# The closing part of an MLP down projection: one row block finished ahead of the other, and a final RMSNorm whose square sums are added up ahead

## The chip, the cores and the metric

The kernel runs on one core of a Trainium2 chip. The metric is the device time of one execution in microseconds (us). The engines are named as in the profile: PE (TensorE), PEld (its weight loads), DVE (VectorE), ACT (ScalarE), POOL (GpSimd) and SP (SyncE, which only starts DMAs here); SPq, ACTq and POOLq are the queues on which these engines start DMAs.

## The reference, cut to what matters

A block of 256 tokens and 2048 channels passes a gated mixer (a linear recurrence beside a banded attention), then a squared-ReLU MLP of 8192 channels, then a last RMSNorm. All is float32. The change lies in the last two lines.

```python
h = h + mixer_block(rms_norm(h, norm_mix_w[l]), ...)
u = rms_norm(h, norm_mlp_w[l])
h = h + jnp.square(jax.nn.relu(u @ w_up[l])) @ w_down[l]
return rms_norm(h, norm_final_w)     # y * rsqrt(mean(y * y) + 1e-6) * w
```

## The kernel before

**Products.** Each float32 operand is split into a high and a low part (`wh`, `wl` for weights), and a product is three matmuls (L135, L136, L137 in `mm3`). The split of a piece of weights, 128x1024, is a cast on ACT (L91) and a subtraction on DVE (L92). The raw piece comes by a DMA on SP's queue (L688 in `piece`) into one of three kinds of buffers: `raw` (six of them), `rawd` (two), `rawp` (three). The split halves have five buffers each (`buf`). SP takes its DMAs in order, so one that waits for its buffer holds those behind it.

**Units.** The MLP is done as a row of `Unit`s. A unit computes two blocks of 512 output columns (n = 0, 1) for both blocks of 128 rows (m = 0, 1): four accumulators c11, c12, c21, c22 in PSUM. The first half of the contraction goes by a scheme with seven block products in place of eight (`product`; pieces A, B, C, D, with sums of raw pieces taken on DVE and by accumulating DMAs on POOL's queue), the second half by "plain" pieces of two contraction blocks each: `plain(n, ks)` for ks = (8,9), (10,11), (12,13), (14,15), each for both m. `LATE` are the last two of these. The order of a unit is written out in `run`; a scheduler places the instructions of every other engine around it.

**The last unit** is `dn32` (`tail=True`): output columns 1024 to 2047 of the down projection, the last quarter of its contraction. Its plain pieces of n = 0 go as in every unit: (12,13) for m = 0 and 1, then (14,15) for m = 0 and 1, then `u.end(0)` calls `done` for m = 0 and m = 1. The pieces of n = 1 then go in three steps: the first 256 columns of m = 1, all 512 of m = 0, the last 256 of m = 1, each step with both LATE pieces and followed by `done`.

**The last norm.** `done` is `out_of`. For the last quarter it adds the accumulator to the residual in `fin[m]` (`evict`, L717, DVE), squares it on ACT with the sum of squares into one column of `ssq3` (L1112, an ACTIVATE and a read of the accumulator), and for n below 3 multiplies by the norm's weights `wf` (L1114, DVE). Here n runs over four blocks of 512 columns; n = 0 and 1 come from unit `dn30`, n = 2 and 3 from `dn32`. When the last block of a row block m is there, DVE adds up the sums (L1118), turns them into a mean (L97), POOL raises it to the power -1/2 (L98), and four blocks are scaled: two on DVE (L1126, L1124, the latter with `wf`) and two on ACT (L1128). Each scaled block is written out by a DMA (L1129), two on SP's queue and two on ACT's.

`finals` (L1133, L1137) runs as a step of unit `dn30`. It loads `wf`, the norm's weights repeated over 128 partitions (1 MB), and the eight 256 KB blocks of the residual into `fin`, all on POOL's queue. In `dn30` ACT also copies the accumulator of product 21 twice (`u_dn`, L748), each time before PE adds to it again.

Of the kernel before, what the change touches and what calls it, by code (L numbers as in the profile page):

```python
# [8 lines left out]
F32 = mybir.dt.float32  # L9
# [3 lines left out]
ALU = mybir.AluOpType  # L13
# [3 lines left out]
P = 128  # L17
# [33 lines left out]
def tile_hybrid_block(  # L51
# [30 lines left out]

    mhalf = const.tile([P, 32], F32, name="mhalf")
    nc.gpsimd.memset(mhalf[:, 0:4], -0.5)
    room = small.tile([P, 56], F32, name="room", tag="room", bufs=1)
    nc.gpsimd.memset(room, 0.0)

    casts, marks = [], []
# [537 lines left out]
    def token(what, pool=None):  # L626
        if pool is not None:
            return pool.tile([P, NC], F32, name=what, tag="t2", bufs=8)
        return tk.tile([P, NC], F32, name=what, tag="t", bufs=TOK)
# [92 lines left out]
    class Unit:  # L722
# [13 lines left out]
        def load_item(self):  # L736

            n, ks = self.items.pop(0)
            self.raw[n, ks] = piece(self.w, f"{self.what}r{n}_{ks[0]}", self.n0 + n * NC, self.kt0 + ks[0], "rawp")

        def bank(self, i):

# [78 lines left out]
    def run(u, then=None):  # L821

        def q():
            if late:
                late.pop(0)()

        def item(x):
            if x and x.items:
                x.load_item()

        if not u.raw:
            u.load("A")
            u.load("B")
            u.load("C")
            u.load("D")
        for _ in range(3 - sum(type(k) is tuple for k in u.raw)):
            item(u)
        at = iter(range(99))
        u.bank("11")
        u.product("11", "A", u.block(0, 0), True)  # L840
        u.begun("21", "11")
        q()
        u.sums("A", "B")
        u.sent("B", "C")
        item(u)
        u.bank("22")
        u.product("22", "A", u.comb(5), True)
        u.begun("12", "22")
        q()
        item(u)  # L850
        u.steps = list(u.make_steps())
        u.step(next(at))
        u.product("12", "C", u.comb(4))
        u.step(next(at))
        u.product("11", "D", u.block(0, 1))
        with ExitStack() as es:
            if u.fresh:
                es.enter_context(tc.issue_after(lows[-1].ins))
            u.sums("A", "C")
        u.sent("D", "A")  # L860
        u.step(next(at))
        u.plain(1, (8, 9))
        item(u)
        u.step(next(at))
        u.product("21", "A", u.comb(2))
        u1 = u.copy(token(f"u1_{u.what}"), "21")
        if then:
            then.load("A")
        u.step(next(at))
        u.plain(1, (10, 11))  # L870
        u.less("12", u1)
        item(u)
        u.step(next(at))
        u.product("21", "B", u.comb(7))
        u2 = u.copy(token(f"u2_{u.what}"), "21")
        if then:
            then.load("B")
            then.load("C")
        u.step(next(at))
        u.plain(0, (8, 9))  # L880
        u.less("22", u2)
        item(u)
        u.step(next(at))
        u.plain(0, (10, 11))
        item(u)
        u.step(next(at))
        u.product("21", "D", u.block(1, 1))
        if then:
            then.load("D")
        u.step(next(at))  # L890
        u.plain(0, (12, 13))
        item(u)
        u.step(next(at))
        u.plain(0, (14, 15))
        marks.clear()
        item(then)
        u.end(0)
        while u.steps:
            u.step(99)

        if u.tail:
            halves = [u.plain(1, ks, ()) for ks in LATE]
            for m, c in ((1, slice(0, T)), (0, slice(0, NC)), (1, slice(T, NC))):
                for h in halves:
                    h(m, c)
                u.done(m, 1, u.c["12"[m] + "2"], c)
            return

        def rest():
            u.plain(1, LATE[1])  # L910
            u.end(1)

        late.append(lambda: u.plain(1, LATE[0]))
        late.append(rest)
# [146 lines left out]
        nc.gpsimd.dma_start(hd[n][m], t)  # L1061
        h1[n][m] = t

    ssq3 = small.tile([P, NM, 5], F32, name="ssq3", tag="ssq3", bufs=1)
    ssum3 = small.tile([P, NM], F32, name="ssum3", tag="ssum")
    rstd3 = const.tile([P, NM], F32, name="rstd3")
    NQ = 4
# [3 lines left out]
    for qd in range(NQ):  # L1071
        last = qd == NQ - 1
        uT, rs, Su, blocks = [], {}, {}, {}

        def turns(c0, uT=uT, rs=rs, Su=Su, blocks=blocks, qd=qd):

            def one(c, m):
                if not m:
                    uT.append(new_act(f"u{qd}{c}"))
                hi, lo = uT[c][:, :, 0, :], uT[c][:, :, 1, :]  # L1080
                tp = transpose4(rs[c, m], f"u{qd}{c}{m}")
                if c < 2:
                    blocks[m, c] = fours(token(f"a{m}{c}_u{qd}"))
                    nc.scalar.copy(blocks[m, c], tp)
                split(hi[:, :, m * P:(m + 1) * P], lo[:, :, m * P:(m + 1) * P], tp)

            return [(c, lambda c=c, m=m: one(c, m)) for c in (c0, c0 + 1) for m in range(NM)] + [
                (c0 + 1, f, 7) for f in ([] if c0 else combos(uT, f"u{qd}", tk, Su, blocks))]

        for c in range(0, 4, 2):  # L1090
            def done(m, n, acc, c=c, rs=rs, qd=qd):
                t = token(f"r{qd}{c}{n}{m}")
                with tc.high_priority(offset=2000):
                    nc.scalar.activation(t, acc, AF.Relu, scale=rstd2[:, m:m + 1])
                nc.scalar.activation(t, t, AF.Square)
                rs[c + n, m] = t

            units.append(Unit(lambda: hT, lambda: Sh, w_up, qd * (FF // NQ) + c * NC, f"up{qd}{c}", done,
                              steps=(lambda turns=turns: turns(0)) if c else (lambda: ()) if qd else (lambda: h_blocks(2)), start=3 if c else 0))

        def out_of(m, n, acc, c=slice(0, NC), last=last, qd=qd):
            if not last:
                t = token(f"y{qd}{n}{m}")
                with tc.high_priority(offset=2000):
                    nc.scalar.copy(t, acc)  # L1105
                nc.gpsimd.dma_start(hd[n][m], t, accum_op=ALU.add)  # L1106
                return
            wf = fin["w"]
            r = fin[m][:, n * NC:(n + 1) * NC]
            evict(r[:, c], acc[:, c])  # L1110
            j = n + (c.start > 0)
            nc.scalar.activation(token(f"ysq_{j}_{m}")[:, c], r[:, c], AF.Square, accum_out=ssq3[:, m, j:j + 1])  # L1112
            if n < 3:
                nc.vector.tensor_tensor(r, r, wf[:, n * NC:(n + 1) * NC], op=ALU.mult)  # L1114
                return
            if c.stop < NC:
                return
            nc.vector.tensor_reduce(ssum3[:, m:m + 1], ssq3[:, m, 0:j + 1], axis=AX.X, op=ALU.add)  # L1118
            rsqrt(rstd3[:, m:m + 1], ssum3[:, m:m + 1], D, 1)
            f = rstd3[:, m:m + 1]  # L1120
            for i in (2, 0, 3, 1):
                t = fin[m][:, i * NC:(i + 1) * NC]
                if i == 3:
                    nc.vector.scalar_tensor_tensor(t, t, f, wf[:, i * NC:(i + 1) * NC], op0=ALU.mult, op1=ALU.mult)  # L1124
                elif i == 2:
                    nc.vector.tensor_scalar(t, t, f, None, op0=ALU.mult)  # L1126
                else:
                    nc.scalar.activation(t, t, AF.Copy, scale=f)  # L1128
                (nc.sync if i > 1 else nc.scalar).dma_start(out[m * P:(m + 1) * P, i * NC:(i + 1) * NC], t)  # L1129

        def finals():
            fin["w"] = apool.tile([P, D], F32, name="wf", tag="act")
            nc.gpsimd.dma_start(fin["w"], bass.AP(tensor=norm_final_w.tensor, offset=norm_final_w.offset, ap=[[0, P], [1, D]]))  # L1133
            for m in range(NM):
                fin[m] = apool.tile([P, D], F32, name=f"fin{m}", tag="act")
                for n in range(4):
                    nc.gpsimd.dma_start(fin[m][:, n * NC:(n + 1) * NC], hd[n][m])  # L1137

        for n0 in (0, 2):
            units.append(Unit(lambda uT=uT: uT, lambda Su=Su: Su, w_down, n0 * NC, f"dn{qd}{n0}",  # L1140
                              lambda m, n, acc, *c, n0=n0, out_of=out_of: out_of(m, n0 + n, acc, *c), kt0=qd * KD,
                              steps=(lambda: ()) if n0 else (lambda turns=turns, last=last: turns(2) + [(3, finals)] * last),
                              start=0, tail=last and n0 == 2))
# [47 lines left out]
```

## Time and profile before

| | us |
|---|---|
| time, median of 3 runs (lowest to highest) | 1399.73 (1399.07 to 1400.38) |
| time of the profiled execution | 1399.67 |
| its span, first to last instruction | 1398.0 |
| PE busy in the span | 1381.4 (99%) |
| DVE, ACT, POOL busy | 1138.2, 922.3, 143.8 |
| first matmul of `dn32`'s plain pieces (12,13) of n = 0 | at 1376.28 |
| last matmul begins | at 1387.21 |

The profiled execution's time stands 1.67 us above its span. Times of single instructions are counted from the span's start. A row of the timeline gives start, duration, engine, line, operation and tiles, how many were merged, and in brackets how long the engine had been idle and what released it. Matmuls overlap: one of 512 columns is shown with 0.39 us, but the next begins 0.23 us after it.

### The profile page before, as it was taken

To read this page: it belongs to the slowest core of one execution; us is meant where nothing else is said; L and a number is where in the kernel's file an instruction comes from. 1 tells how busy PE (TensorE), PEld (TensorE's weight loads), DVE (VectorE), ACT (ScalarE), POOL (GpSimd) and SP (SyncE) were. 2 spreads that over 40 slices of the span, in tenths; PEclk is the share of its full clock that TensorE was granted. 3 is DMA by queue.
4 is the path that set the end of the run, shared out by engine and by line. 5 is a ranking of instruction groups with operands and counts; after the bars stand their busy time and mean duration, and the time that the engine had idled before them with its cause. 6 is when DMAs were issued, how large, how long until landed. Compare 5 with 4: busy or idle time off the path is not lost.

```text
span 1398.0 us, 18644 instructions
## 1 busy us (share of the span) xinstructions
PE 1381.4 (99%) x6550; PEld 1144.4 (82%) x6550; DVE 1138.2 (81%) x1431; ACT 922.3 (66%) x1192; POOL 143.8 (10%) x228
## 2 busy tenths in 40 slices
PE   9999999999999999999999999999999999999997
PEld 7889888878777888888888888888888888888885
DVE  7897997976978785687998987889877888879885
ACT  6774764665676674346777776778666876668764
POOL 2000001010100000001211001100011001010200
PEclk9999999999999999999999999999999999999999
DMA  9755455775769897658988889998899888999883
GB/s 318 242 168 161 154 166 181 225 269 162 183 187 271 251 278 225 193 169 268 283 244 275 252 268 267 274 280 240 249 295 299 248 230 254 281 279 275 267 245 114
DMA packets 124078, 331.62 MB, mean 237 GB/s; under 512 B 11072, under 2 KB 11840, under 8 KB 123600
## 3 DMA queue, kind: packets, MB, share of 16 engines
q1 hardware_dynamic: 103264, 264.80, 55.1%
q0 software_dynamic: 19568, 64.04, 23.3%
q10 hardware_dynamic: 1152, 1.60, 0.4%
q8 instruction: 51, 0.84, 0.2%
q14 instruction: 43, 0.35, 0.1%
HBM read 271.67 MB, written 10.49 MB: 202 GB/s over the span
## 4 chain that ended last, share of the span: by engine, by line
PE 90%; DVE 4%; DMA 3%; issue 1%; ACT 1%; POOL 0%; SPq 0%; POOLq 0%; ACTq 0%; DVEq 0%
PE acc_ak L177 2%; PE acc_aq L177 2%; PE acc_hf L177 2%; PE ps L414 1%; PE acc_ak L182 1%; PE acc_hq L177 1%; PE tp_u L108 1%; PE acc_ga0c L135 1%; PE acc_hg L136 1%; PE acc_bb L136 1%; PE acc_hg L135 1%; PE acc_ba L136 1%; PE acc_bb L137 1%; PE acc_ba L137 1%; PE acc_hg L137 1%
## 5 line engine op out<-in xcount | busy, mean ns | idle before, releaser
L177 PE MATMUL acc_hf<-act_x,wh_hf 128*128 128x512 f32 x128 | 41.0, 402 | 1.0 <-DVE f L190 1.0
L177 PE MATMUL acc_aq<-act_x,wh_aq 128*128 128x512 f32 x128 | 41.6, 406 | 0.0
L177 PE MATMUL acc_hq<-act_x,wh_hq 128*128 128x512 f32 x128 | 40.7, 399 | 0.0
L177 PE MATMUL acc_ak<-act_x,wh_ak 128*128 128x512 f32 x128 | 40.0, 396 | 0.1
L91 ACT CAST wh_bb<-raw_bb 128x1024 fp32r<-128x1024 f32 x16 | 16.9, 1054 | 23.3 <-PE acc_ba L137 17.7
L92 DVE TENSOR_TENSOR wl_bb<-raw_bb,wh_bb 128x1024 fp32r<-128x1024 f32 x16 | 19.6, 1223 | 14.8 <-ACT wh_bb L91 14.8
L91 ACT CAST wh_ba<-raw_ba 128x1024 fp32r<-128x1024 f32 x16 | 16.8, 1052 | 20.9 <-PE acc_bb L137 13.8
L92 DVE TENSOR_TENSOR wl_ba<-raw_ba,wh_ba 128x1024 fp32r<-128x1024 f32 x16 | 19.6, 1223 | 12.6 <-ACT wh_ba L91 12.6
L91 ACT CAST wh_aq<-raw_aq 128x1024 fp32r<-128x1024 f32 x16 | 16.8, 1050 | 19.0 <-PE acc_hg L137 8.8
L92 DVE TENSOR_TENSOR wl_aq<-raw_aq,wh_aq 128x1024 fp32r<-128x1024 f32 x16 | 19.6, 1223 | 11.4 <-ACT wh_aq L91 9.4
L182 PEld LDWEIGHTS acc_hq<-act_x,wl_hq 128*128 128x128 f32 x128 | 23.4, 188 | 6.1 <-DVE wl_hq L92 0.9
L182 PEld LDWEIGHTS acc_hf<-act_x,wl_hf 128*128 128x128 f32 x128 | 23.4, 188 | 6.1 <-DVE wl_hf L92 0.9
L182 PEld LDWEIGHTS acc_aq<-act_x,wl_aq 128*128 128x128 f32 x128 | 23.5, 188 | 5.4 <-issue 0.5
L182 PEld LDWEIGHTS acc_ak<-act_x,wl_ak 128*128 128x128 f32 x128 | 23.5, 188 | 5.3
L92 DVE TENSOR_TENSOR wl_hf<-raw_hf,wh_hf 128x1024 fp32r<-128x1024 f32 (+2 forms) x21 | 20.3, 967 | 7.8 <-ACT wh_hf L91 7.7
L91 ACT CAST wh_hf<-raw_hf 128x1024 fp32r<-128x1024 f32 (+1 forms) x19 | 16.9, 890 | 14.3 <-PE acc_hg L137 6.0
L182 PE MATMUL acc_aq<-act_x,wl_aq 128*128 128x256 f32 x128 | 25.9, 284 | 0.0
L92 DVE TENSOR_TENSOR wl_ak<-raw_ak,wh_ak 128x1024 fp32r<-128x1024 f32 x16 | 19.5, 1221 | 7.7 <-ACT wh_ak L91 7.7
L135 PE MATMUL acc_hi<-wh_hi,act_x 128*128 128x512 f32 x64 | 25.8, 403 | 0.0
L92 DVE TENSOR_TENSOR act_u<-tp_u,act_u 128x512 fp32r<-128x512 f32 x32 | 21.9, 685 | 4.7 <-ACT act_u L91 4.2
L135 PE MATMUL acc_hg<-wh_hg,act_x 128*128 128x512 f32 x64 | 25.7, 401 | 0.0
L1106 POOL DMA_DIRECT2D hd<-y x24 | 25.4, 1137 | 1.9 <-ACT y L1105 1.8
(1922 smaller groups left out, 5248.0 us busy)
## 6 DMA issues: line engine op xcount, KB each, us to landing
raw_hi<-in_w_in_n_dram SPq DMA_DIRECT2D x16, 512.0 KB, 4.4
raw_hg<-in_w_in_n_dram SPq DMA_DIRECT2D x16, 512.0 KB, 3.9
raw_aq<-in_w_in_t_dram SPq DMA_DIRECT2D x16, 512.0 KB, 4.3
raw_ak<-in_w_in_t_dram SPq DMA_DIRECT2D x16, 512.0 KB, 3.8
raw_ba<-in_w_branch_a_dram SPq DMA_DIRECT2D x16, 512.0 KB, 4.5
raw_bb<-in_w_branch_b_dram SPq DMA_DIRECT2D x16, 512.0 KB, 4.6
raw_hf<-in_w_in_t_dram SPq DMA_DIRECT2D x12, 512.0 KB, 3.9
raw_hq<-in_w_in_t_dram SPq DMA_DIRECT2D x12, 512.0 KB, 4.4
```

The lines of the kernel that those rows point to most:

```text
L91: casts[:] = [(copy or nc.scalar.copy)(hi, src)]
L92: return nc.vector.tensor_tensor(lo, src, hi.bitcast(F32), op=ALU.subtract)
L108: nc.tensor.transpose(tp[:, j, :], src[:, j * P:(j + 1) * P], ident)
L135: nc.tensor.matmul(acc, hi, wh, start=first, stop=False, skip_group_check=True)
L136: nc.tensor.matmul(acc, hi, wl, start=False, stop=False, skip_group_check=True)
L137: nc.tensor.matmul(acc, lo, wh, start=False, stop=last, skip_group_check=True)
L177: nc.tensor.matmul(acc[:, cb, :], wh[:, cb * P:(cb + 1) * P], r.rearrange("p u t -> p (u t)"), start=kt == 0, stop=last)
L182: nc.tensor.matmul(acc[:, cb, 0:T], wl[:, cb * P:(cb + 1) * P], r[:, 0, :], start=False, stop=False)
L414: nc.tensor.matmul(ps[:, m, :], klf[:, a * P:(a + 1) * P], qrf[:, a * 192:(a + 1) * 192], start=True, stop=True)
L1106: nc.gpsimd.dma_start(hd[n][m], t, accum_op=ALU.add)
```

## The change

In the last unit the four LATE pieces, two of n = 0 and two of n = 1, are all split ahead, and then PE goes in five steps: n = 0 for m = 0, n = 1 for m = 0, the first 256 columns of n = 1 for m = 1, n = 0 for m = 1, the last 256 columns of n = 1 for m = 1. Each step takes its two LATE pieces and ends in `done`. So m = 0 is complete after the second step; its scaling and its writes stand between the work of m = 1 on ACT's, DVE's and SP's queues.

The two LATE raw pieces of n = 1 go into `raw` buffers, and their loads stand ahead of the last three `rawp` loads on SP's queue.

`ssq3` has one more column, set to 2048 * 1e-6 by POOL near the start of the kernel. The sums of squares that are there when block n = 2 is done are added up then (DVE), and POOL adds the last one and takes the power itself. The mean step on DVE goes. Since the factor is now (sum + 2048 eps)^(-1/2), the weights `wf` are multiplied once by the square root of 2048, on ACT, in unit `dn30`: ACT's order has it (128x2048) right in front of the first `u_dn` copy.

Seven of the eight output writes go on SP's queue; the last one, block 1 of m = 1, on ACT's. `room` is a filler that keeps the addresses of the small tiles. PE has the same matmuls as before.

```diff
         def load_item(self):
             n, ks = self.items.pop(0)
-            self.raw[n, ks] = piece(..., "rawp")
+            self.raw[n, ks] = piece(..., "raw" if self.tail and n and ks in LATE else "rawp")
...
         u.product("21", "D", u.block(1, 1))
         if then:
             then.load("D")
+        if u.tail:
+            ends = [[u.plain(n, ks, ()) for ks in LATE] for n in range(2)]
+            for m, n, c in ((0, 0, slice(0, NC)), (0, 1, slice(0, NC)), (1, 1, slice(0, T)), (1, 0, slice(0, NC)), (1, 1, slice(T, NC))):
+                for h in ends[n]:
+                    h(m, c)
+                u.done(m, n, u.c["12"[m] + "12"[n]], c)
+            return
+
...
-        if u.tail:
-            halves = [u.plain(1, ks, ()) for ks in LATE]
-            for m, c in ((1, slice(0, T)), (0, slice(0, NC)), (1, slice(T, NC))):
-                for h in halves:
-                    h(m, c)
-                u.done(m, 1, u.c["12"[m] + "2"], c)
-            return
...
             evict(r[:, c], acc[:, c])
-            j = n + (c.start > 0)
+            j = n + 1 + (c.start > 0)
             nc.scalar.activation(token(f"ysq_{j}_{m}")[:, c], r[:, c], AF.Square, accum_out=ssq3[:, m, j:j + 1])
+            if n == 2:
+                with tc.high_priority(offset=3000):
+                    nc.vector.tensor_reduce(ssum3[:, m:m + 1], ssq3[:, m, 0:4 + m], axis=AX.X, op=ALU.add)
             if n < 3:
                 nc.vector.tensor_tensor(r, r, wf[:, n * NC:(n + 1) * NC], op=ALU.mult)
-                return
-            if c.stop < NC:
-                return
-            nc.vector.tensor_reduce(ssum3[:, m:m + 1], ssq3[:, m, 0:j + 1], axis=AX.X, op=ALU.add)
-            rsqrt(rstd3[:, m:m + 1], ssum3[:, m:m + 1], D, 1)
-            f = rstd3[:, m:m + 1]
+            elif c.stop == NC:
+                f = rstd3[:, m:m + 1]
+                nc.gpsimd.tensor_tensor(f, ssq3[:, m, j:j + 1], ssum3[:, m:m + 1], op=ALU.add)
+                nc.gpsimd.tensor_tensor(f, f, mhalf[:, 0:1], op=ALU.pow)
...
-                (nc.sync if i > 1 else nc.scalar).dma_start(out[m * P:(m + 1) * P, i * NC:(i + 1) * NC], t)
+                    (nc.scalar if m and i == 1 else nc.sync).dma_start(out[m * P:(m + 1) * P, i * NC:(i + 1) * NC], t)
 
         def finals():
+            nc.gpsimd.memset(ssq3[:, :, 0:1], D * EPS)
             fin["w"] = apool.tile([P, D], F32, name="wf", tag="act")
             nc.gpsimd.dma_start(fin["w"], ...)
+            nc.scalar.activation(fin["w"], fin["w"], AF.Copy, scale=D ** 0.5)
```

More of the change, by code (lines that the diff above doesn't have):

```diff
@@ L84, in tile_hybrid_block @@
     nc.gpsimd.memset(mhalf[:, 0:4], -0.5)
-    room = small.tile([P, 56], F32, name="room", tag="room", bufs=1)
+    room = small.tile([P, 88], F32, name="room", tag="room", bufs=1)
     nc.gpsimd.memset(room, 0.0)
@@ L738, in load_item @@
             n, ks = self.items.pop(0)
-            self.raw[n, ks] = piece(self.w, f"{self.what}r{n}_{ks[0]}", self.n0 + n * NC, self.kt0 + ks[0], "rawp")
+            self.raw[n, ks] = piece(self.w, f"{self.what}r{n}_{ks[0]}", self.n0 + n * NC, self.kt0 + ks[0],
+                                    "raw" if self.tail and n and ks in LATE else "rawp")
         def bank(self, i):
@@ L1062, in h_out @@
         h1[n][m] = t
-    ssq3 = small.tile([P, NM, 5], F32, name="ssq3", tag="ssq3", bufs=1)
+    ssq3 = small.tile([P, NM, 6], F32, name="ssq3", tag="ssq3", bufs=1)
     ssum3 = small.tile([P, NM], F32, name="ssum3", tag="ssum")
@@ L1116, in out_of @@
-            if c.stop < NC:
-                return
-            nc.vector.tensor_reduce(ssum3[:, m:m + 1], ssq3[:, m, 0:j + 1], axis=AX.X, op=ALU.add)
-            rsqrt(rstd3[:, m:m + 1], ssum3[:, m:m + 1], D, 1)
-            f = rstd3[:, m:m + 1]
[L1121 to L1129, printed above, removed]
+            elif c.stop == NC:
+                f = rstd3[:, m:m + 1]
+                nc.gpsimd.tensor_tensor(f, ssq3[:, m, j:j + 1], ssum3[:, m:m + 1], op=ALU.add)
+                nc.gpsimd.tensor_tensor(f, f, mhalf[:, 0:1], op=ALU.pow)
+                for i in (2, 0, 3, 1):
+                    t = fin[m][:, i * NC:(i + 1) * NC]
+                    if i == 3:
+                        nc.vector.scalar_tensor_tensor(t, t, f, wf[:, i * NC:(i + 1) * NC], op0=ALU.mult, op1=ALU.mult)
+                    elif i == 2:
+                        nc.vector.tensor_scalar(t, t, f, None, op0=ALU.mult)
+                    else:
+                        nc.scalar.activation(t, t, AF.Copy, scale=f)
+                    (nc.scalar if m and i == 1 else nc.sync).dma_start(out[m * P:(m + 1) * P, i * NC:(i + 1) * NC], t)
```

## The prediction

> **What bounds the kernel now.** I read the page first: how long the span is, who is busy, and the chain that ended last.
>
> ```profile
> span 1398.0 us, 18644 instructions
> PE 1381.4 (99%) x6550; PEld 1144.4 (82%) x6550; DVE 1138.2 (81%) x1431; ACT 922.3 (66%) x1192; POOL 143.8 (10%) x228
> PE 90%; DVE 4%; DMA 3%; issue 1%; ACT 1%; POOL 0%; SPq 0%; POOLq 0%; ACTq 0%; DVEq 0%
> ```
>
> PE sets the time nearly everywhere, and the change gives it the same matmuls. So there are two questions: does PE still run without a gap up to its last matmul, and how long is what follows it? That end I read in the timeline, from the last two evictions on.
>
> ```profile
> 1381.92 0.69 DVE L717 TENSOR_TENSOR fin<-acc_dn32c,fin 128x512 f32<-128x512 f32 x1 [0.67 <-PE acc_dn32c L137]
> 1386.10 0.69 DVE L717 TENSOR_TENSOR fin<-acc_dn32c,fin 128x512 f32<-128x512 f32 x1 [1.72 <-PE acc_dn32c L137]
> 1387.21 0.28 PE L137 MATMUL acc_dn32c<-wh_dn32r,act_u 128*128 128x256 f32 x1
> 1387.53 0.42 DVE L717 TENSOR_TENSOR fin<-acc_dn32c,fin 128x256 f32<-128x256 f32 x1 [0.74 <-PE acc_dn32c L137]
> 1387.87 0.14 DVE L1118 TENSOR_REDUCE ssum<-ssq 128x1 f32<-128x4 f32 x1
> 1388.29 0.58 POOL L98 TENSOR_TENSOR rstd<-ms,mhalf 128x1 f32<-128x1 f32 x1 [31.86 <-DVE ms L97]
> 1388.31 0.19 ACT L1112 ACTIVATION_READ_ACCUMULATOR ysq<-fin 128x1 f32 x1
> 1388.90 1.33 ACT L1128 ACTIVATE fin<-fin,rstd 128x512 f32<-128x512 f32 x2 [0.41 <-POOL rstd L98]
> 1389.30 0.75 DVE L1124 SCALAR_TENSOR_TENSOR fin<-fin,rstd,wf 128x512 f32<-128x512 f32 x1
> 1389.41 3.06 SPq L1129 DMA_DIRECT2D out_dram<-fin  x4
> 1389.96 0.15 DVE L1118 TENSOR_REDUCE ssum<-ssq 128x1 f32<-128x5 f32 x1
> 1390.15 0.15 DVE L97 TENSOR_SCALAR ms<-ssum 128x1 f32<-128x1 f32 x1
> 1390.38 0.55 POOL L98 TENSOR_TENSOR rstd<-ms,mhalf 128x1 f32<-128x1 f32 x1 [1.52 <-DVE ms L97]
> 1390.97 1.33 ACT L1128 ACTIVATE fin<-fin,rstd 128x512 f32<-128x512 f32 x2 [0.74 <-POOL rstd L98]
> 1390.97 0.49 DVE L1126 TENSOR_SCALAR fin<-fin,rstd 128x512 f32<-128x512 f32 x1 [0.67 <-POOL rstd L98]
> 1391.72 0.99 ACTq L1129 DMA_DIRECT2D out_dram<-fin  x2
> ```
>
> The two row blocks end together. The last eviction of m = 0 is at 1386.10, that of m = 1 at 1387.53. The reduction of m = 0 stands behind that eviction on DVE (1387.87), so its factor is used only from 1388.90. The last sum of squares of m = 1 is read at 1388.31 + 0.19 = 1388.50, but DVE is busy scaling m = 0 until its reduction can go at 1389.96; mean and power follow, and m = 1 is scaled from 1390.97. I call the time from which a row block is scaled U: U was 1388.90 for m = 0, 1390.97 for m = 1. All eight writes start after 1389.4. The next view is their landing, for the first one and for the last two, and the DMA busy share and rate from 1388 to 1399 in 40 slices of 0.275 us.
>
> ```profile
> L1129 SPq DMA_DIRECT2D out_dram<-fin x1: 344/344/344, 1389.4 to 1389.4; - x1
> DMA to landing us min/median/max: 2.3/2.3/2.3
> L1129 SPq DMA_DIRECT2D out_dram<-fin x1: 332/332/332, 1392.1 to 1392.1; - x1
> L1129 ACTq DMA_DIRECT2D out_dram<-fin x1: 373/373/373, 1392.3 to 1392.3; - x1
> DMA to landing us min/median/max: 4.6/4.6/4.6
> DMA  0000000079999999999999999998540000000000
> GB/s 0 0 0 0 0 0 0 0 276 402 410 410 402 387 320 425 387 395 395 343 320 231 350 395 365 328 395 313 216 156 8 0 0 0 0 0 0 0 0 0
> DMA packets 1152, 2.10 MB, mean 191 GB/s; under 512 B 128, under 2 KB 128, under 8 KB 1152
> ```
>
> The first write needed 2.3 us, the last 4.6 us: the DMA engines are full from slice 8 (1390.2) to slice 28 and empty at 1396.3. So the writes of m = 1 queue behind those of m = 0. The last lands at 1392.3 + 4.6 = 1396.9, 0.6 us after the last packet, and the span ends 1.1 us after that, at 1398.0, which is U + 7.03 for m = 1.
>
> **The change part by part.** *PE's order.* PE does the same matmuls. Before it finished n = 0 for both m (24 matmuls of 512 columns, 0.23 us apart, as the 5.6 us from 1376.28 to the eviction at 1381.92 show) before it needed the LATE pieces of n = 1; now it needs them after 12, at 1376.28 + 2.7 = 1379.0. The last subtractions of those pieces:
>
> ```profile
> 1374.84 2.60 DVE L92 TENSOR_TENSOR wl_dn32r<-rawp_dn32r,wh_dn32r 128x1024 fp32r<-128x1024 f32 x2 [1.49 <-ACT wh_dn32r L91]
> 1350.60 1.22 DVE L92 TENSOR_TENSOR wl_dn32p12C<-raw_dn32C,wh_dn32p12C 128x1024 fp32r<-128x1024 f32 x1
> 1357.15 14.68 SPq L688 DMA_DIRECT2D rawp_dn32r<-in_w_down_dram  x5
> ```
>
> They end at 1377.44, 1.6 us early: cost nothing, and should the cover go, PE slips by what exceeds 1.6. That also holds for the raw loads, which now go into `raw` buffers ahead of three `rawp` loads in SP's order. The `raw` buffers that they take are those of piece C, last read by the subtraction at 1350.60 to 1351.82; the `rawp` load behind them started at 1357.15. So SP is through 5 us early and holds nothing back. PE's end stays: 1387.5.
>
> *The end of m = 0.* Its last eviction comes 24 matmuls after 1376.28, where m = 1's n = 0 was evicted before: 1381.92, not 1386.10. From the start of an eviction to the read sum took 1387.53 to 1388.50 for 256 columns, about 1.4 for 512; with add and power on POOL U is near 1384.3. ACT's two scalings (1.33) end near 1385.7 and stand ahead of m = 1's squares in ACT's queue, DVE's two (0.49 and 0.75) near 1385.5 ahead of its evictions: the next to be late would be the eviction at 1386.10, so both fit. Four writes of m = 0 are done by about 1389.5, before m = 1 begins to write.
>
> *The end of m = 1.* The reduction moves to 1387.87, beside the square; the mean (0.15) goes; the wait for DVE behind m = 0 goes. POOL gets an add. No row shows an add on POOL; the nearest are these.
>
> ```profile
> L84 POOL MEMSET mhalf<- 128x4 f32 x1 | 0.1, 101 | 0.0
> 141.53 0.69 POOL L98 TENSOR_TENSOR ro<-ms,mhalf 128x2 f32<-128x2 f32 x1 [2.98 <-DVE ms L97]
> 740.45 1.22 DVE L92 TENSOR_TENSOR wl_up00r<-rawp_up00r,wh_up00r 128x1024 fp32r<-128x1024 f32 x1
> 740.62 1.61 POOL L98 TENSOR_TENSOR rstd<-ms,mhalf 128x2 f32<-128x2 f32 x1 [13.18 <-DVE ms L97]
> ```
>
> Its bounds are 0.10 (a memset) and 0.58 (the power); I take 0.20, nearer to the memset, since the power's extra work is what an add lacks. Chain: read at 1388.50, 0.09 to POOL (as from the mean's end, 1388.20, to 1388.29), add 0.20, 0.05 between them, power 0.55, 0.03 to ACT: U = 1389.42, against 1390.97, 1.55 earlier.
>
> Beside it DVE multiplies m = 1's block 2 by `wf`, about 1387.95 to 1388.65. The power took 0.69 with DVE idle and 1.61 beside a DVE subtraction of two SBUF operands; here only the first 0.07 us of the add lies beside one, so I price that at 0.05, inside the bounds. The Trainium skill says as much against this change: in its GPSIMD Engine Reference, Specifications, GpSimd's SBUF interfaces are shared with VectorE and contend with VectorE instructions that have two SBUF inputs. The 1.61 agrees; by that rule U would be later by what the multiplication overlaps.
>
> *The writes.* The first transfer of m = 0 began 1.3 after its U (1390.2). For m = 1 the issue order gives the same start, then 1.05 MB, half the 2.10, at the 395 GB/s of slices 9 to 18 takes 2.65, landing 0.6, end 1.1: U + 5.65 in place of U + 7.03, 1.4 less. That three of its writes share SP's queue costs nothing, since an issue takes 0.34 and its transfer 0.66.
>
> *`wf` on ACT.* One activation of 128x2048, ahead of the copy that PE's product 21 B waits for.
>
> ```profile
> L1133 POOL DMA_DIRECT2D wf<-in_norm_final_w_dram x1: 588/588/588, 1310.5 to 1310.5; - x1
> DMA to landing us min/median/max: 11.4/11.4/11.4
> L212 ACT ACTIVATE xr<-xr 128x2048 f32<-128x2048 f32 x2 | 3.8, 1920 | 1.6 <-DMA xr<-in_x_dram 1.6
> 1322.08 0.59 ACT L748 COPY u_dn<-acc_dn30c 128x512 f32<-128x512 f32 x1 [0.30 <-PE acc_dn30c L137]
> 1324.60 0.39 PE L135 MATMUL acc_dn30c<-wh_dn30p21B,S_u 128*128 128x512 f32 x1
> DMA to landing us min/median/max: 10.9/13.9/15.9
> ```
>
> `wf` lands at 1321.9. ACT then scales for 1.92, to 1323.9, and copies for 0.59, to 1324.5; PE needs the copy at 1324.60. It just fits: I charge 0.1, between 0 and 0.4. What is queued behind on ACT are casts for matmuls that PE comes to only after 21 B. POOL's memset of the new column, 0.1, comes near the start and delays nobody.
>
> Sum: -1.55 - 1.4 + 0.05 + 0.1 = -2.8. Span 1395.2, with the 1.67 outside it 1396.9; the profiled execution stands 0.06 under the median of 1399.73, which I let go. A measurement of this kernel can tell about 0.2%, 2.8 us, from no change: the line lies at 1396.93, on the forecast itself.
>
> **The rivals.** *Quicker writes.* If m = 1's last write, issued at U + 1.37, lands like the first one of before, in 2.3 to 3.0, the end is U + 4.8 to 5.5: 1394.2 to 1394.9, time 1395.9 to 1396.6. For it: the queues are empty then. Against it: 1.05 MB needs 2.65 anyhow.
>
> *POOL's pair is slow, or m = 1's writes gain nothing from an empty queue.* An add of 0.58 and a power stretched to 1.0 beside DVE put U at 1390.2; or the writes need as long as m = 0's did (its last landing 5.3 after U, at 1394.2). Either gives back 0.7 to 0.8: 1397.7. For it: the 1.61. Against it: DVE is idle during the power.
>
> *The change trades the end for a stall in `dn30`, slower than before.* The mechanism is `wf`'s landing: ACT waits for it in order, with the copy and all casts behind. PE slips one for one beyond 0.15 us of slack. The eight loads queued right behind `wf` took 10.9 to 15.9 us. If `wf` takes 15.9 in place of 11.4, PE loses 4.35 and the time is 1396.9 + 4.3 = 1401.2. It decides from a landing of 14.4 us on. Against it: nothing ahead of `wf` changes.
>
> *The change does not do what it says*: the last pieces of n = 1 are late at 1379.0, PE waits, and m = 0 ends no earlier. It needs the 1.6 us of cover to go; 1397.5 at one us beyond. I leave it in the second rival.
>
> **How the numbers follow.** Forecast 0.46, its own range 1396.2 to 1397.6 from the add's bounds (-0.1, +0.4) and the stall's (0 to 0.4), half on each side of the line; quicker writes 0.29, all faster; slow POOL or slow writes 0.16, all within; late `wf` 0.09, of which 0.05 past 1402.5 (a landing of over 17 us, beyond the rows) and 0.04 within. Faster 0.23 + 0.29 = 0.52, same 0.23 + 0.16 + 0.04 = 0.43, slower 0.05. The range leaves out the late `wf` and the outermost of the quick writes: 1395.6 to 1398.6.
>
> **What would show it.** Right: PE's last matmul still near 1387.2; m = 0's last eviction near 1381.9, its writes landed before 1390; POOL's add at 1388.6 of 0.1 to 0.3; ACT scaling m = 1 from 1389.4; DMA empty by 1394. Wrong: a gap of PE before product 21 B in `dn30`, or in the last 11 us; a POOL pair of over 1 us; m = 1's last landing over 4 us after its issue.

## The result, and the profile after

The changed kernel took 1396.28 us (median of 15 runs, 1395.22 to 1399.54), the kernel before 1399.07 us (median of 15 runs, 1397.33 to 1400.38). The ratio is 0.9982, 95% interval 0.9975 to 0.9989: faster by some 2.8 us (the interval allows 1.5 to 3.5). That is clear of no change, but 0.18% falls just short of the 0.2% that the prediction drew as its line, and the interval covers that line.

The profiled execution has a span of 1395.6 us against 1398.0. The page's span and the shares of its chain of waits:

```profile
span 1395.6 us, 18652 instructions
PE 89%; DVE 4%; DMA 3%; issue 3%; ACT 1%; POOL 0%; SPq 0%; POOLq 0%; ACTq 0%; DVEq 0%
```

The timeline of the end, as shown for the kernel before:

```profile
1381.98 0.69 DVE L717 TENSOR_TENSOR fin<-acc_dn32c,fin 128x512 f32<-128x512 f32 x1 [0.48 <-PE acc_dn32c L137]
1383.52 0.18 POOL L1121 TENSOR_TENSOR rstd<-ssq,ssum 128x1 f32<-128x1 f32 x1 [27.16 <-ACT ysq L1113]
1383.78 0.58 POOL L1122 TENSOR_TENSOR rstd<-rstd,mhalf 128x1 f32<-128x1 f32 x1
1384.39 1.34 ACT L1130 ACTIVATE fin<-fin,rstd 128x512 f32<-128x512 f32 x2 [0.96 <-POOL rstd L1122]
...
1387.27 0.28 PE L137 MATMUL acc_dn32c<-wh_dn32r,act_u 128*128 128x256 f32 x1
1387.59 0.42 DVE L717 TENSOR_TENSOR fin<-acc_dn32c,fin 128x256 f32<-128x256 f32 x1 [0.74 <-PE acc_dn32c L137]
1388.00 0.68 DVE L1118 TENSOR_TENSOR fin<-fin,wf 128x512 f32<-128x512 f32 x1
1388.37 0.19 ACT L1113 ACTIVATION_READ_ACCUMULATOR ysq<-fin 128x1 f32 x1
1388.64 0.19 POOL L1121 TENSOR_TENSOR rstd<-ssq,ssum 128x1 f32<-128x1 f32 x1 [4.28 <-ACT ysq L1113]
1388.90 0.55 POOL L1122 TENSOR_TENSOR rstd<-rstd,mhalf 128x1 f32<-128x1 f32 x1
1389.49 1.33 ACT L1130 ACTIVATE fin<-fin,rstd 128x512 f32<-128x512 f32 x2 [0.93 <-POOL rstd L1122]
1389.89 0.75 DVE L1126 SCALAR_TENSOR_TENSOR fin<-fin,rstd,wf 128x512 f32<-128x512 f32 x1
```

PE still makes up 89% of the chain. From the first matmul of product 21 B in `dn30` to its last matmul it takes 62.61 us in both kernels, so it neither gained nor lost there; that the last matmul begins at nearly the same time (1387.27 and 1387.21) is chance, as the other profiles below show. Row block m = 0 is evicted for the last time at 1381.98 and scaled from 1384.39, while PE still works on m = 1. The last sum of m = 1 is read at 1388.56, and ACT and DVE scale m = 1 from U = 1389.49, in place of 1390.97.

The view of the tile `out_dram`: the last two issues, and the time from issue to landing:

```profile
L1131 ACTq DMA_DIRECT2D out_dram<-fin x1: 377/377/377, 1390.9 to 1390.9; - x1
L1131 SPq DMA_DIRECT2D out_dram<-fin x1: 414/414/414, 1390.9 to 1390.9; - x1
DMA to landing us min/median/max: 3.2/3.4/3.6
```

The DMA view from 1388 to 1395, busy share of the DMA engines in tenths and rate, in slices of 0.175 us:

```profile
DMA  9963000000000000699999999999999530000000
GB/s 328 351 234 117 0 0 0 0 0 0 0 0 0 0 0 0 269 398 386 410 433 410 386 386 398 316 374 398 386 328 339 223 141 12 0 0 0 0 0 0
```

The DMA engines run empty at 1388.7, before m = 1 writes (twelve slices are zero). Its 1.05 MB move from 1390.85 to 1393.8; the last lands at 1394.5, and the span ends 1.1 us later, at U + 6.11 in place of U + 7.03.

### The profile page after: what moved, and what is told of

It is laid out like the page before. It is cut to its first block, busy times and chain, and to the rows that moved or that the text cites. A ratio compares the mean times of both kernels' runs of the same rounds, so it can differ in the third digit from the quotient of the medians.

```text
span 1395.6 us, 18652 instructions
## 1 busy us (share of the span) xinstructions
PE 1381.4 (99%) x6550; PEld 1143.6 (82%) x6550; DVE 1139.1 (82%) x1429; ACT 925.4 (66%) x1193; POOL 144.4 (10%) x231
## 4 chain that ended last, share of the span: by engine, by line
PE 89%; DVE 4%; DMA 3%; issue 3%; ACT 1%; POOL 0%; SPq 0%; POOLq 0%; ACTq 0%; DVEq 0%
PE acc_ak L177 2%; PE acc_hf L177 2%; PE acc_aq L177 2%; PE acc_hq L177 2%; PE ps L414 1%; PE acc_ak L182 1%; PE tp_u L108 1%; PE acc_hg L136 1%; PE acc_bb L136 1%; PE acc_hg L135 1%; PE acc_hg L137 1%; PE acc_ba L136 1%; PE acc_ba L137 1%; PE acc_bb L137 1%; PE acc_bb L135 1%
## 5 line engine op out<-in xcount | busy, mean ns | idle before, releaser
L98 POOL TENSOR_TENSOR ro<-ms,mhalf 128x2 f32<-128x2 f32 x8 | 5.9, 738 | 189.8 <-DVE ms L97 189.8
```

The lines of the kernel that those rows point to most:

```text
L98: nc.gpsimd.tensor_tensor(dst, ms, mhalf[:, :width], op=ALU.pow)
```

## The experiments

Spans of single executions differ by more than the effects here: the first matmul of product 21 B in `dn30` came between 1322.29 and 1324.66 in the profiles below, and these two extremes are e6_queues and the changed kernel, which differ only in the queues of the last writes. It follows the matmul before it by 0.22 to 0.23 us in all ten, and from it to the last matmul all ten have the same 62.61 us. So the spread lies ahead of product 21 B, and each kernel is read from its own last matmul, L. U is where m = 1 is scaled on ACT; these numbers are of the profiled executions, in us. The span is printed to 0.1, so its two differences hold to 0.05; four kernels with the same writes (changed, e4, e7, e9) show a span - U of 5.97 to 6.11, and less than that 0.14 is not read as a difference. The last column is the ratio of each kernel's runs to those of the kernel before, with its 95% interval.

| kernel | span | L | U - L | span - U | span - L | runs' ratio |
|---|---|---|---|---|---|---|
| before | 1398.0 | 1387.21 | 3.76 | 7.03 | 10.79 | 1 |
| changed | 1395.6 | 1387.27 | 2.22 | 6.11 | 8.33 | 0.9982 (0.9975 to 0.9989) |
| e1_order | 1394.0 | 1385.62 | 2.33 | 6.05 | 8.38 | 0.9984 (0.9975 to 0.9992) |
| e2_chain | 1397.1 | 1386.86 | 3.96 | 6.28 | 10.24 | 1.0001 (0.9991 to 1.001) |
| e3_nowrite0 | 1395.4 | 1385.38 | 3.76 | 6.26 | 10.02 | 0.9992 (0.9983 to 1.0001) |
| e4_nowf | 1393.8 | 1385.50 | 2.22 | 6.08 | 8.30 | 0.9986 (0.9977 to 0.9995) |
| e6_queues | 1393.1 | 1384.90 | 2.22 | 5.98 | 8.20 | 0.9979 (0.997 to 0.9988) |
| e7_rawp | 1394.3 | 1386.11 | 2.22 | 5.97 | 8.19 | 0.9983 (0.9974 to 0.9992) |
| e9_wftwice | 1394.9 | 1386.65 | 2.22 | 6.03 | 8.25 | 0.9974 (0.9964 to 0.9985) |
| e8_best | 1395.2 | 1386.38 | 2.76 | 6.06 | 8.82 | 0.9986 (0.9977 to 0.9995) |

By the runs, e2_chain and e3_nowrite0 cannot be told from the kernel before, and the others, all faster than it, cannot be told from the changed kernel. What parts them is the end, span - L.

**PE's order alone.** The diff of `run` and `load_item` put into the kernel before; `out_of` and `finals` as they were.

```diff
 before.py
+        if u.tail:
+            ends = [[u.plain(n, ks, ()) for ks in LATE] for n in range(2)]
+            ...
-        if u.tail:
-            halves = ...
```

> The kernel before with PE's new order and the new raw buffers alone; the norm's chain (sum, mean and power, 1/2048 and eps in the mean), the unscaled weights and the four queues of writes stay as before. Theory A (the gain is the order: m = 0 is out of DVE's and the writes' way, and the rewritten chain adds little): DVE is free when m = 1's last sum is read at about 1388.55, so reduction 0.15, mean 0.15, power 0.55 and their steps give U = 1389.6 for m = 1, against 1389.49 in the changed kernel and 1390.97 before; span about 1395.7. Rival B (the sums added ahead and the add on POOL carry a good part of the 1.5 us): U of 1390.1 or later, span 1396.3 or more.

Its timeline from the last matmul on:

```profile
1385.62 0.28 PE L137 MATMUL acc_dn32c<-wh_dn32r,act_u 128*128 128x256 f32 x1
1386.72 0.19 ACT L1113 ACTIVATION_READ_ACCUMULATOR ysq<-fin 128x1 f32 x1
1386.94 0.16 DVE L1119 TENSOR_REDUCE ssum<-ssq 128x1 f32<-128x5 f32 x1
1387.13 0.15 DVE L97 TENSOR_SCALAR ms<-ssum 128x1 f32<-128x1 f32 x1
1387.37 0.56 POOL L98 TENSOR_TENSOR rstd<-ms,mhalf 128x1 f32<-128x1 f32 x1 [4.26 <-DVE ms L97]
1387.95 1.33 ACT L1129 ACTIVATE fin<-fin,rstd 128x512 f32<-128x512 f32 x2 [1.04 <-POOL rstd L98]
```

The sum is read at 1386.91 and DVE's old reduction starts at 1386.94, 0.03 us later, since nothing of m = 0 stands before it; in the kernel before it waited 1.46 us (1388.50 to 1389.96). U is L + 2.33, against L + 2.22 with the new chain. The order alone brings 2.41 of the 2.46 us between the two ends (span - L), which is all of it as far as the profiles can tell. Theory A holds, rival B falls.

**The chain, the weights and the queues alone.** The changed kernel with `run` and `load_item` of before; the sums of m = 1 are added up after the first half of its last block.

```diff
 after.py
-            if n == 2:
+            if n == 2 + m and not c.start:
```

> The changed kernel with PE's order and the raw buffers of before: only the norm's chain, the scaled weights and the queues of the writes are new (the sums of m = 1 are added up after the first half of its last block). Theory A: nothing is gained, since both row blocks end together: ACT's order has m = 0's two scalings, which wait for POOL's power at about 1388.45, ahead of m = 1's last square, so that square starts near 1389.7 and U of m = 1 is about 1391.2; the writes still queue up; span 1398.0 to 1398.5. Rival B: U of m = 1 about 1389.5 to 1389.8, span 1396.5 to 1397.4.

```profile
1386.86 0.28 PE L137 MATMUL acc_dn32c<-wh_dn32r,act_u 128*128 128x256 f32 x1
1388.15 1.33 ACT L1129 ACTIVATE fin<-fin,rstd 128x512 f32<-128x512 f32 x2 [0.96 <-POOL rstd L1121]
1389.70 0.19 ACT L1112 ACTIVATION_READ_ACCUMULATOR ysq<-fin 128x1 f32 x1
1389.96 0.19 POOL L1120 TENSOR_TENSOR rstd<-ssq,ssum 128x1 f32<-128x1 f32 x1 [1.84 <-ACT ysq L1112]
1390.82 1.33 ACT L1129 ACTIVATE fin<-fin,rstd 128x512 f32<-128x512 f32 x2 [0.93 <-POOL rstd L1121]
```

The DMA engines' busy share from 1388.1 to 1397.1, in slices of 0.225 us:

```profile
DMA  0000005999999999989999999999995520000000
```

As theory A had it, ACT scales m = 0 ahead of m = 1's last square, whose sum is read only at 1389.89, and U is L + 3.96, later than before's L + 3.76. The end came 0.55 us sooner in this profile nevertheless, which theory A missed. m = 0 is scaled from L + 1.29 in place of L + 1.69, so the writes start 0.40 us sooner, and the DMA engines never run empty between the two row blocks; that accounts for most of the 0.55. Over 11 runs the ratio was 1.0001: no gain that could be measured. This holds for the order that ACT was given here; m = 1's last square ahead of m = 0's scalings was not run.

**The kernel before without m = 0's writes.**

```diff
 before.py
+                if m:
                     (nc.sync if i > 1 else nc.scalar).dma_start(out[...], t)
```

> The kernel before with the four writes of m = 0 left out (rows 0 to 127 of the output are not written). It measures the queue of m = 1's writes behind m = 0's by itself. Theory A: U of m = 1 stays 1390.97 and the span ends 6.1 us after it, as in the changed kernel, in place of 7.03: 1397.1, 0.9 less. Rival C (the end after U is latency, not a queue): 1398.0 within 0.2.

```profile
1385.38 0.28 PE L137 MATMUL acc_dn32c<-wh_dn32r,act_u 128*128 128x256 f32 x1
1389.14 1.33 ACT L1128 ACTIVATE fin<-fin,rstd 128x512 f32<-128x512 f32 x2 [0.74 <-POOL rstd L98]
```

U - L is before's 3.76 to the digit, and the span ends 6.26 after U in place of 7.03. So 0.77 us of the old end was m = 1's writes standing behind m = 0's; rival C, pure latency, falls. That is 0.15 less than the 0.92 that the changed kernel gained there, about what two profiles of the same writes can differ by.

**Without the scaling of `wf`.** The ACT line in `finals` taken out.

> The changed kernel without the scaling of the final norm's weights on ACT (the output lacks the factor sqrt(2048)). Theory A: the copy for product 21 B ended at 1324.1 in the changed kernel, 0.55 us before PE needs it, so the scaling costs nothing and the span stays within 0.3 of the changed kernel's; PE's first matmul of 21 B comes at the same distance after the last one before it (0.23 us). Rival D (part of the gain is given back there): PE's part up to 21 B is 0.1 to 0.4 us shorter.

U - L is the same 2.22, the end within 0.03, and 21 B to L the same 62.61. These would not show a wait right ahead of 21 B; the distance of its first matmul from the one before does, and it is 0.23 us with the scaling and without it:

```profile
1322.66 0.39 PE L137 MATMUL acc_dn30c<-wh_dn30r,act_u 128*128 128x512 f32 x1
1322.89 0.39 PE L135 MATMUL acc_dn30c<-wh_dn30p21B,S_u 128*128 128x512 f32 x1
```

The scaling is hidden whole. In the changed kernel the copy that PE waits for ended at 1324.11, 0.55 before PE's first matmul of 21 B:

```profile
1321.74 1.91 ACT L1137 ACTIVATE wf<-wf 128x2048 f32<-128x2048 f32 x1
1323.55 0.56 ACT L749 COPY u_dn<-acc_dn30c 128x512 f32<-128x512 f32 x1
1324.43 0.39 PE L137 MATMUL acc_dn30c<-wh_dn30r,act_u 128*128 128x512 f32 x1
1324.66 0.39 PE L135 MATMUL acc_dn30c<-wh_dn30p21B,S_u 128*128 128x512 f32 x1
```

**`wf` scaled twice.** A second activation, times 1.0, behind the first.

> The changed kernel with a second pass of 128x2048 over the weights on ACT (times 1.0), behind the first. It measures the cover of the scaling. Theory A: ACT's copy for product 21 B ends 1.85 us later, at 1325.95, and PE, which needs it at 1324.66, waits 1.3 to 1.4 us; nothing else changes; span 1.3 to 1.4 more than the changed kernel's. Rival D: PE does not wait for that copy, or makes it up before the end: under 0.5 more.

```profile
1321.12 1.91 ACT L1137 ACTIVATE wf<-wf 128x2048 f32<-128x2048 f32 x1
1322.93 0.56 ACT L749 COPY u_dn<-acc_dn30c 128x512 f32<-128x512 f32 x1
1325.30 1.91 ACT L1138 ACTIVATE wf<-wf 128x2048 f32<-128x2048 f32 x1
1327.11 0.56 ACT L749 COPY u_dn<-acc_dn30c 128x512 f32<-128x512 f32 x1
```

Theory A missed: the scheduler put the second pass behind the first copy, into the next hole of ACT. 21 B to L stayed 62.61, and the distance ahead of 21 B 0.22. So this measured two holes in place of the price of an overrun; the price of a late `wf` was not measured by any run.

**The queues of before.** `(nc.sync if i > 1 else nc.scalar)` for both m.

> The changed kernel with the writes on the queues of before (blocks 2 and 3 on SP's, 0 and 1 on ACT's, for both m). In the changed kernel SP's third write of m = 1 started 0.2 us after its data were there, since each issue holds SP 0.33 to 0.46 us. Theory A: with two writes on each queue the last one starts at U + 1.37 as now and the third 0.2 us sooner; span 0 to 0.2 less. Rival E (issuing on ACT delays ACT's scaling or its squares): span 0.2 to 0.5 more.

U - L is 2.22, so rival E falls. span - U is 5.98 against 6.11, which agrees with theory A, but kernels with the changed kernel's own queues show 5.97 to 6.11 too, so a gain is not shown. Moving seven writes to SP's queue gains nothing that could be measured.

**The last raw pieces in `rawp` buffers.** `load_item` as before.

> The changed kernel with the last two raw pieces of n = 1 in the rawp buffers as before, so that their loads go last on SP's queue. Theory A: they land by 1372 and 1376, their subtractions end by 1376.2 and 1378.5, and PE needs them at 1379.1 and 1380.4: PE has no gap and the span is that of the changed kernel within 0.3. Rival F (the early loads are needed): a gap of PE of over 0.2 us at the first matmul of n = 1 for m = 0, and the span is longer by it.

21 B to L 62.61, U - L 2.22, span - L 8.19: PE never waits for these pieces, and the early loads gain nothing. Rival F falls.

**Further: block 3 multiplied early, smaller first write.**

```diff
 after.py
-            if n < 3:
-                nc.vector.tensor_tensor(r, r, wf[:, n * NC:(n + 1) * NC], op=ALU.mult)
-            elif c.stop == NC:
+            wn = wf[:, n * NC:(n + 1) * NC]
+            nc.vector.tensor_tensor(r[:, c], r[:, c], wn[:, c], op=ALU.mult)
+            if n == 3 and c.stop == NC:
...
+                for e, q, lo, hi in ((0, 0, 1024, 1280), (1, 1, 0, 512), (0, 0, 1280, 1792), (0, 0, 1792, 2048), (1, 1, 512, 1024)):
...
```

A first digit of 1 has the columns scaled on ACT, of 0 on DVE; a second digit of 1 has them written from ACT's queue for m = 1, all else from SP's.

> The changed kernel, taken further: block 3 too is multiplied by the weights in DVE's idle time before the factor is there, so all three DVE scalings are of the short kind; DVE scales in pieces of 256, 512 and 256 columns (block 2's first half first), SP writes these three, ACT scales and writes blocks 0 and 1. Theory A (after U the end is first issue, then 1.05 MB, then landing): the first write starts at U + 0.3 in place of U + 0.52 and the last at U + 1.37; U as in the changed kernel; span 0.2 to 0.5 less. Rival G (more and smaller writes cost more than the early start gives): 0 to 0.3 more.

```profile
1382.86 0.68 DVE L1118 TENSOR_TENSOR fin<-fin,wf 128x512 f32<-128x512 f32 x1
1382.88 1.10 POOL L1122 TENSOR_TENSOR rstd<-rstd,mhalf 128x1 f32<-128x1 f32 x1
1385.79 0.43 DVE L1118 TENSOR_TENSOR fin<-fin,wf 128x256 f32<-128x256 f32 x1 [0.75 <-ACT ysq L1113]
1386.13 1.01 DVE L717 TENSOR_TENSOR fin<-acc_dn32c,fin 128x512 f32<-128x512 f32 x2
1386.38 0.28 PE L137 MATMUL acc_dn32c<-wh_dn32r,act_u 128*128 128x256 f32 x1
1387.68 1.02 DVE L1118 TENSOR_TENSOR fin<-fin,wf 128x512 f32<-128x512 f32 x2
1387.79 0.19 ACT L1113 ACTIVATION_READ_ACCUMULATOR ysq<-fin 128x1 f32 x1
1388.05 0.36 POOL L1121 TENSOR_TENSOR rstd<-ssq,ssum 128x1 f32<-128x1 f32 x1 [4.06 <-ACT ysq L1113]
1388.49 0.62 POOL L1122 TENSOR_TENSOR rstd<-rstd,mhalf 128x1 f32<-128x1 f32 x1
1389.14 1.33 ACT L1126 ACTIVATE fin<-fin,rstd 128x512 f32<-128x512 f32 x2 [1.17 <-POOL rstd L1122]
```

Worse by 0.49 at the end (span - L 8.82), though the runs' ratio cannot tell it from the changed kernel; and not by rival G: span - U is 6.06, as it was, but U is 0.54 later. Two things did it. The last sum is read at L + 1.60 in place of L + 1.29, because the added multiplication of m = 1's first half waits for ACT's square (DVE idle 0.75 us) and m = 1's last evictions stand behind it. And POOL's add and power, beside the multiplications, take 0.36 and 0.62 where they took 0.19 and 0.55, so U comes 1.16 after the sum in place of 0.93. m = 0's power, with a multiplication of 0.68 us beside its start, took 1.10 in place of 0.58. Theory A's gain after U did not come either: the last write landed at U + 4.7 in place of U + 5.0, but the span ended 1.4 us after it in place of 1.1. Why, no run shows.

No version beat the changed kernel by more than the runs can tell. The order alone is as good as the whole change.

## Why the prediction was right

The time forecast was 1396.9, the range 1395.6 to 1398.6; measured 1396.28. The 0.6 between them is the kernel before, whose median was 1399.07 over 15 runs where three had given 1399.73. The forecast difference, -2.8, met the measured one of the medians, -2.79, and that is luck: between the two profiled ends (span - L) it was -2.46. The mechanism was right, one term was too large, and two small charges that did not come offset part of it. The prediction gave 0.52 to a gain beyond its line of 0.2% and 0.43 to one within it; the measured 0.18% is the second, on the edge. Two slips in its arithmetic: its rows for `wf` add up to 1324.4, not 1324.5, and the bounds that it names for its own range reach down to 1396.7, not 1396.2, so less than half of that range lay beyond the line.

- *PE's order costs PE nothing, m = 0 ends near 1381.9*: so it was (1381.98, and 62.61 us from 21 B to L as before), and m = 0's writes were out of the queue some 2.1 us before those of m = 1 began.
- *U of m = 1 1.55 earlier*: 1.54 counted from L. The chain was right row by row: add 0.19 (0.20 taken), power 0.55, U at 0.93 after the read sum (0.92 taken). But the working did not part the causes. Experiment e1 does: 1.43 of it comes from the order, since DVE no longer stands behind m = 0; only 0.11 is the new chain. The add and its extra step take back most of what the mean and the reduction cost.
- *Writes 1.4 less*: 0.92. This is the mis-sized term. 1.05 MB took 2.95 us where 2.65 was taken at a steady 395 GB/s: slices of 316 to 374 GB/s in between account for about 0.1, and most of the rest is the tail (223, 141, 12), which a steady rate leaves out. Start and landing were 0.05 and 0.1 later than taken. The mechanism stands: e3 gives 0.77 for m = 0's writes alone.
- *`wf` on ACT 0.1*: nothing. The room left was 0.55 us: the weights were there when ACT came free at 1321.74, and the operations follow each other some 0.1 sooner than their durations add up.
- *POOL beside DVE 0.05*: not to be seen with the 0.04 us of overlap that there was. e8 shows what a longer overlap costs. The Trainium skill's rule (GPSIMD Engine Reference, Specifications: contention with VectorE instructions that have two SBUF inputs) agrees with the 1.10 against 0.58.
- *The rivals*: quicker writes did not come (the last two landed after 3.2 to 3.6 us, not 2.3 to 3.0). This landing is what parts that rival from the forecast, since 1396.28 lies within its 1395.9 to 1396.6 too. A slow POOL pair, late pieces and a stall in `dn30` did not come either. Slow writes, the other half of the second rival, came in part: m = 1's last write landed 5.0 us after its U, where the forecast had 4.55 and that rival 5.3, and m = 0's, into empty DMA engines too, landed 5.0 after theirs. But an empty queue did gain 0.92. What a late `wf` costs stays open: nothing here made it late.

## What to carry to other kernels

When two blocks finish together and share the engines and the queue of an epilogue, let one finish early inside the other's matmuls: the order of equal work was worth 2.4 us here, and rewriting the epilogue's arithmetic on top of it 0.1. Do one part of a change at a time before crediting it; two parts of this one (queues, early loads) were worth nothing that could be measured. Where executions differ by more than the effect, measure from an event that all share, as from the last matmul here.

## What the runs showed of the hardware that was not expected

A power of one column on POOL took 0.55 to 0.58 us with DVE nearly idle, and 1.10 where a DVE multiplication of two SBUF operands ran beside its first 0.66 us (e8); an add of one column 0.18 to 0.19, and 0.36 beside such multiplications. Beside an eviction, which has one of its operands in PSUM, m = 0's add took 0.18, as alone. SP's issue of a write took 0.33 to 0.35 us where issues were 0.6 us or more apart and 0.37 to 0.46 where they followed closely. Four writes of 256 KB into empty DMA engines moved at 355 GB/s on the mean, not at the some 400 of their first half. From the last landing to the end of the span it took 1.0 us (e6) to 1.4 us (e8), and no run shows why it differs.
